# SSD mixer of a hybrid decoder trunk: the gate's product from PSUM, its norm in six calls, decayed x by ScalarE, and transposed b in one bank with c·b

## The chip, the core and the metric

One NeuronCore of a Trainium2 chip runs the whole program. It has TensorE (PE, matmuls, results in PSUM banks), VectorE (DVE), ScalarE (ACT), GpSimd (POOL, which does not touch PSUM here) and SyncE (SP, which issues DMAs here). Each engine runs its own instructions in order and waits for the others on semaphores. The metric is the device time of one execution in microseconds (us); lower is better.

## The reference

All arrays are float32. 1040 tokens (16 learned ones, then 1024) pass a Mamba-2 SSD mixer, a conv gated FFN, stick-breaking attention and a second FFN. The change is in the mixer:

```python
z, xbc, dt_raw = split(u @ w_in)
xbc = silu(causal_dwconv(xbc, conv_w, conv_b))
xs, b_in, c_in = split(xbc)            # 4 groups of 8 heads of 64; state 128
dt = softplus(dt_raw + dt_bias)
xdt = x_c * dt_c                       # per chunk and head
cb = einsum('bclgn,bcsgn->bgcls', c_c, b_c)
y_diag = einsum('bgcls,bgecls,bcsgep->bclgep', cb, decay_in, xdt)
decay_to_end = exp(a_cs[..., -1:] - a_cs)
chunk_states = einsum('bclgn,bgecl,bclgep->cbgepn', b_c, decay_to_end, xdt)
...                                    # scan over chunks, y_off from the states
y = y_diag + y_off + xs * d_skip
hg = y * silu(z)                       # the gate
hg = hg * rsqrt(mean(hg * hg over a group of 512) + eps)
out = (hg * gate_g) @ w_out
```

## The kernel before

Activations lie with channels on the partitions and tokens along the free axis, in three token tiles of 348, 348 and 344 (`TT`). The input projection is done by blocks of 128 channels: a *tile* is one block and one token tile, 24 matmuls into one PSUM bank (`project`, L153 to L155: each product is split into high and low parts). The bank is `pj`, of the pools `mm` (two banks) and `ex` (one), so that a bank comes back after three tiles. A tile of x, b or c then gets its conv: a first step by ScalarE (L275) and three by VectorE (L278), and Silu (L459). A tile of the gate gets Silu into an SBUF tile `z` (L491), the product with y (L498, `product`), the square (L503) and the sum of squares (L507, L509).

The SSD itself goes by four groups of heads (0 to 3) and nine chunks of up to 116 tokens (0 to 8). For a chunk, `ssd_decays` loads the cumulated decays into D and E by DMA, subtracts eight times on VectorE (L573) and takes the exponential on ScalarE (L574); `ssd_front` makes c·b (`cb`, L589), the transposed x (`px`, L592), the masked `cbm` (L595), `xdt` (L597), the decayed product D (L598), the transposed b (`pb`, L602) with its copy `bk` (L604), and the decayed x, `xde` (L606); `ssd_back` makes the chunk's state S from `bk` and `xde` (L619, L626) and y (L631, L633, L635). `cb`, `pb`, y and the norm's `ms` share the pool `sm` of three banks (a tag each allocation takes in turn), `px` and S the pool `lg` of two.

`mixer` writes the order by hand for all engines but the DMA queues: between a chunk's front and its back it puts the tiles of the next group's projection and of this group's gate (`stream`), about two a chunk in groups 0 and 3, and three or four in groups 1 and 2. Each chunk's decays are computed after the second tile of the chunk before. The gate of group g runs in group g+1; in that group, after its four blocks, `norm` is called at three tiles in a row, once for each token tile: `rstd` sums over partitions into a bank `ms` (L186), takes Ln and Exp on ScalarE (L189, L190) and one Newton step on VectorE (L191 to L194, of which L192 reads `ms`); `gate_norm` scales four blocks (L520).

Of the kernel before, what the change touches and what calls it, by code (L numbers as in the profile page):

```python
# [8 lines left out]
F32 = mybir.dt.float32  # L9
# [4 lines left out]
P = 128  # L14
# [52 lines left out]
class Trunk:  # L67
# [109 lines left out]
        self.tc.keep_in_program_order(self.nc.scalar.preload_act_table_set("natural_log_exp_and_others"))  # L177


    def rstd(self, accs, n, width, y=None, table=True):  # L180
        nc = self.nc
        if table:
            self.ln_exp()
        ps = self.sm("ms")
        for i, acc in enumerate(accs):
            nc.tensor.matmul(ps[:, :n], self.ones, acc[:, :n], start=i == 0, stop=i == len(accs) - 1)  # L186
        b = accs[0]
        y = self.tmp("y")[:, :n] if y is None else y
        nc.scalar.activation(y, ps[:, :n], AF.Ln, scale=1.0 / width)  # L189
        nc.scalar.activation(y, y, AF.Exp, scale=-0.5)  # L190
        nc.vector.tensor_tensor(b[:, :n], y, y, op=ALU.mult)  # L191
        nc.vector.tensor_tensor(b[:, :n], b[:, :n], ps[:, :n], op=ALU.mult)  # L192
        nc.vector.tensor_scalar(b[:, :n], b[:, :n], -0.5 / width, 1.5, op0=ALU.mult, op1=ALU.add)
        nc.vector.tensor_tensor(y, y, b[:, :n], op=ALU.mult)  # L194
        return y
# [185 lines left out]
    def dt_path(self, ps, r9, cp):  # L381

        nc, a = self.nc, self.a
        H, C = HEADS, 9 * HEADS
        heads = cp.tile([P, 2, H], F32, tag="heads", name="heads")
        nc.gpsimd.dma_start(heads.rearrange("p i h -> p (i h)"), a["heads"].to_broadcast([P, 2 * H]))
        aneg = heads[:, 1]
        self.tc.keep_in_program_order(nc.scalar.activation(aneg, aneg, AF.Exp))
        nc.vector.tensor_scalar(aneg, aneg, -1.0, None, op0=ALU.mult)

        G = 3 * H
        rows = self.tmp("rows")
        nc.gpsimd.memset(rows[:G, TT[2][1] : 3 * CB], 0.0)
        for j, (_, n) in enumerate(TT):
            nc.scalar.activation(rows[j * H : j * H + H, :n], ps[j * H : j * H + H, :n], AF.Copy)
        pv = self.sm("dt")
        for i in range(3):
            nc.tensor.transpose(pv[:CB, i * G : i * G + G], rows[:G, i * CB : i * CB + CB], self.ident[:G, :G])
        self.cols = cp.tile([P, 3, 9, H], F32, tag="cols", name="cols")
        R = slice(0, CB), slice(0, C)  # L400
        dt, acs, dte = (self.cols[:CB, i].rearrange("p c h -> p (c h)") for i in range(3))
        e, q, s, v = (self.tmp("dt")[R] for _ in range(4))
        tt, stt, ts = nc.vector.tensor_tensor, nc.vector.scalar_tensor_tensor, nc.vector.tensor_scalar

        bias = heads[:CB, 0].unsqueeze(1).to_broadcast([CB, 9, H])
        v3 = v.rearrange("p (c h) -> p c h", h=H)
        tt(v3, pv[R].rearrange("p (c h) -> p c h", h=H), r9[:CB].rearrange("p i j -> p (i j)").unsqueeze(2).to_broadcast([CB, 9, H]), op=ALU.mult)
        tt(v3, v3, bias, op=ALU.add)
        nc.scalar.activation(e, v, AF.Abs)
        nc.scalar.activation(e, e, AF.Exp, scale=-1.0)  # L410
        ts(q, e, 0.5, 1.0, op0=ALU.mult, op1=ALU.add)
        nc.vector.reciprocal(q, q)
        tt(s, e, q, op=ALU.mult)
        tt(e, s, s, op=ALU.mult)
        ts(q, e, 1.0 / (13 * 4**6), None, op0=ALU.mult)
        for c in (5, 4, 3, 2, 1):
            stt(q, q, 1.0 / ((2 * c + 1) * 4**c), e, op0=ALU.add, op1=ALU.mult)
        stt(q, q, 1.0, s, op0=ALU.add, op1=ALU.mult)
        stt(dt, v, 0.0, q, op0=ALU.max, op1=ALU.add)

        last = self.cols[:CB, 0, 8]
        nc.gpsimd.affine_select(out=last, in_=last, compare_op=ALU.is_ge, fill=0.0, base=CH[8][1] - 1, pattern=[[0, H]], channel_multiplier=-1)
        yield 1

        tt(e.rearrange("p (c h) -> p c h", h=H), self.cols[:CB, 0], aneg[:CB].unsqueeze(1).to_broadcast([CB, 9, H]), op=ALU.mult)
        pa, pe = self.sm("acs"), self.sm("end")
        nc.tensor.matmul(pa[R], self.past[:CB, :CB], e, start=True, stop=True)
        nc.tensor.matmul(pe[:, :C], self.ones[:CB, :], e, start=True, stop=True)
        nc.vector.tensor_copy(acs, pa[R])
        self.cd = cp.tile([P, 9, H], F32, tag="cd", name="cd")  # L430
        nc.scalar.activation(self.cd.rearrange("p c h -> p (c h)"), pe[:, :C], AF.Exp)
        tt(dte, pe[R], acs, op=ALU.subtract)
        nc.scalar.activation(dte, dte, AF.Exp)
        yield 2

        self.acs_d = self.dp.tile([9, H, CB], F32, tag="acs_d", name="acs_d")
        self.ea_d = self.dp.tile([9, H, CB], F32, tag="ea_d", name="ea_d")
        pr = self.sm("rows")
        for i in range(3):
            nc.tensor.transpose(pr[:G, i * CB : i * CB + CB], self.cols[:CB, 1, 3 * i : 3 * i + 3].rearrange("p c h -> p (c h)"), self.ident[:CB, :CB])  # L440
        ea = self.tmp("ea")
        nc.vector.tensor_copy(rows[:G, : 3 * CB], pr[:G, : 3 * CB])
        nc.scalar.activation(ea[:G, : 3 * CB], pr[:G, : 3 * CB], AF.Exp)
        for j in range(3):
            for d, t in ((self.acs_d, rows), (self.ea_d, ea)):
                nc.sync.dma_start(d[3 * j : 3 * j + 3].rearrange("c h l -> h c l"),
                                  t[j * H : j * H + H, : 3 * CB].rearrange("h (c l) -> h c l", l=CB))
        yield 3
# [29 lines left out]
        return [block(DI + (4 * g + q) * P, 4 * g + q) for q in range(4)] + [  # L478
            block(2 * DI + g * P, 16 + g), block(2 * DI + (GROUPS + g) * P, 20 + g)]

    def gate_group(self, u, g, x, acc, later):

        nc = self.nc
        tt = nc.vector.tensor_tensor
# [1 line left out]
        def block(q):  # L486
            def tile(w, j):
                s0, n = TT[j]
                ps = self.project(w, u, j, 0, bank=self.ex if j == 2 else None)
                z = self.tmp("z")  # L490
                nc.scalar.activation(z[:, :n], ps[:, :n], AF.Silu)  # L491
                self.settle()
                later(j, lambda: product(j, z))

            def product(j, z):
                s0, n = TT[j]
                xq = x[q][:, s0 : s0 + n]
                tt(xq, xq, z[:, :n], op=ALU.mult)  # L498
                self.open.append(lambda: square(j, z))

            def square(j, z):
# [10 lines left out]

        return [block(q) for q in range(4)]

    def gate_norm(self, g, x, acc, j):
        s0, n = TT[j]
        r = self.rstd([acc.pop(j)], n, DI // GROUPS)
        for q in range(4):
            xq = x[q][:, s0 : s0 + n]
            self.nc.vector.scalar_tensor_tensor(xq, xq, self.par("gate_norm", 4 * g + q), r, op0=ALU.mult, op1=ALU.mult)  # L520
# [7 lines left out]
    def stream(self, blocks, w0=None):  # L528
# [3 lines left out]
        todo = []  # L532
        for src, f in blocks:
            if src is None:
                for j in range(3):
                    calls[3 * len(todo) + 1 + j] = lambda f=f, j=j: f(j)
            else:
                todo.append((src, f))
# [41 lines left out]
    def ssd_front(self, g, x, bt, ct, c, dk, pool):  # L580
# [4 lines left out]
        t0, n = CH[c]  # L585
        cc = 3 * (c % 3) + c // 3
        e = t0 + n
        pcb = self.sm("cb")
        nc.tensor.matmul(pcb[:n, :n], bt[:, t0:e], ct[:, t0:e], start=True, stop=True)  # L589
        px = self.lg("px")  # L590
        for q in range(4):
            nc.tensor.transpose(px[:n, q * P : q * P + P], x[q][:, t0:e], self.ident)  # L592
        px = px[:n].rearrange("p (h d) -> p h d", h=GH)
        cbm = pool.tile([P, CB], F32, tag="cbm", name=self.nm("cbm"), bufs=2)
        tt(cbm[:n, :n], pcb[:n, :n], self.past[:n, :n], op=ALU.mult)  # L595
        xdt = pool.tile([P, GH, 64], F32, tag="xdt", name=self.nm("xdt"), bufs=2)
        tt(xdt[:n], px, self.cols[:n, 0, cc, h0 : h0 + GH].unsqueeze(2).to_broadcast([n, GH, 64]), op=ALU.mult)  # L597
        tt(dk, dk, cbm[:n, :n].unsqueeze(1).to_broadcast([n, GH, n]), op=ALU.mult)  # L598
        bk = xde = None
        if c < 8:  # L600
            pb = self.sm("pb")
            nc.tensor.transpose(pb[:n, :P], bt[:, t0:e], self.ident)  # L602
            bk = pool.tile([P, P], F32, tag="bk", name=self.nm("bk"), bufs=2)
            nc.scalar.activation(bk[:n], pb[:n, :P], AF.Copy)  # L604
            xde = pool.tile([P, GH, 64], F32, tag="xde", name=self.nm("xde"), bufs=2)
            nc.gpsimd.tensor_tensor(xde[:n], xdt[:n], self.cols[:n, 2, cc, h0 : h0 + GH].unsqueeze(2).to_broadcast([n, GH, 64]), op=ALU.mult)  # L606
        return xdt, xde, bk

    def ssd_back(self, g, x, c, dk, ce, xdt, xde, bk, state, pool):
# [29 lines left out]
    def mixer(self, mx):  # L639
# [5 lines left out]
        with self.tc.tile_pool(name="ssd", bufs=3) as pool:  # L645
# [8 lines left out]
                    waiting.append((j, f))  # L654

            def gate(g):
                def norm(j):
                    self.gate_norm(g, rows[g], accs[g], j)
                    if j == 2 and g < 2:
                        yd[g] = self.spill(rows[g][:4], f"y{g}_d")  # L660
                return self.gate_group(u, g, rows[g], accs[g], later if g == 3 else lambda j, f: f()) + [(None, norm)]

            into = lambda g: self.in_group(u, g, rows[g])
            blocks = into(1) + gate(0) + into(2) + gate(1) + into(3) + gate(2) + gate(3)
# [861 lines left out]
```

## Time and profile before

| | us |
|---|---|
| median of 3 runs | 3060.58 |
| runs from, to | 3060.25, 3062.45 |
| the profiled execution | 3064.0 |
| its span, first to last instruction | 3062.3 |
| TensorE busy | 2895.1 |
| VectorE busy | 2333.7 |
| ScalarE busy | 1650.2 |
| GpSimd busy | 1421.5 |

Line numbers are those of the kernel before. An engine is busy while an instruction of its own runs; waits are inferred from semaphore events. PEclk is the share of full speed that TensorE's clock was granted. The SSD groups run from 150 to 696 us of the span, and what follows is the output projection, the FFNs and the attention.

### The profile page before, as it was taken

How to read it: one execution, taken by the hardware profiler on the slowest of the kernel's cores; microseconds unless marked ns; L12 is line 12 of the kernel's file. 1: busy time of each engine (PE TensorE's matmuls, PEld its weight loads, DVE VectorE, ACT ScalarE, POOL GpSimd, SP SyncE). 2: the span in 40 equal slices, each digit the busy share in tenths (PEclk: the TensorE clock that was granted, in tenths of full speed). 3: DMA queues.
4: the chain of work that ended last, by engine and by line, in shares of the span. 5: the costliest groups of instructions: out<-in, count | busy, mean ns of one | idle time of the engine just before them, and what ended most of it. 6: DMA issues, size and time to landing. Idle time of an engine off the chain costs nothing. (4 is left out here: it accounts for less than half of the span.)

```text
span 3062.3 us, 58683 instructions
## 1 busy us (share of the span) xinstructions
PE 2895.1 (95%) x22535; PEld 2776.6 (91%) x22535; DVE 2333.7 (76%) x4030; ACT 1650.2 (54%) x3403; POOL 1421.5 (46%) x1289
## 2 busy tenths in 40 slices
PE   5999999989998999998999999999898999998997
PEld 2999898979998999998999999999797999998996
DVE  3686868885458888788966888888759878878874
ACT  3555545553245555554324888878635655565332
POOL 1154434452325766657643222223325666666741
PEclk8999999999998999999999999999998999999998
DMA  3333333324221222234132222221431222225231
GB/s 113 106 93 95 103 88 105 105 70 139 65 89 56 78 77 78 82 114 165 49 126 80 62 63 64 67 62 48 146 110 57 82 82 77 75 87 180 76 98 56
DMA packets 123220, 273.41 MB, mean 89 GB/s; under 512 B 13468, under 2 KB 53020, under 8 KB 122940
## 3 DMA queue, kind: packets, MB, share of 16 engines
q1 hardware_dynamic: 117622, 258.54, 27.3%
q10 hardware_dynamic: 4054, 6.56, 0.6%
q8 instruction: 177, 2.90, 0.4%
q0 software_dynamic: 1264, 4.57, 0.4%
q14 instruction: 103, 0.84, 0.1%
HBM read 201.25 MB, written 53.45 MB: 83 GB/s over the span
## 5 line engine op out<-in xcount | busy, mean ns | idle before, releaser
L153 PE MATMUL pj<-uh,wh 128*128 128x348 f32 (+2 forms) x1536 | 505.4, 329 | 9.0 <-ACT bk L604 6.2
L154 PE MATMUL pj<-ul,wh 128*128 128x348 f32 (+2 forms) x1536 | 497.6, 324 | 0.0
L155 PE MATMUL pj<-uh,wl 128*128 128x348 f32 (+2 forms) x1536 | 494.9, 322 | 0.7 <-POOL wl L1147 0.7
L154 PE MATMUL p<-bl,fh 128*128 128x262 f32 x1408 | 401.2, 285 | 14.0 <-DVE bl L814 14.0
L153 PE MATMUL p<-bh,fh 128*128 128x262 f32 x1408 | 402.2, 286 | 1.6 <-ACT fh L845 1.1
L155 PE MATMUL p<-bh,fl 128*128 128x262 f32 x1408 | 399.7, 285 | 0.0
L846 POOL TENSOR_TENSOR fl<-x,fh 128x1024 fp32r<-128x1024 f32 x88 | 212.7, 2418 | 353.0 <-ACT fh L845 276.3
L147 POOL TENSOR_TENSOR wl<-w,wh 128x1024 fp32r<-128x1024 f32 (+2 forms) x80 | 164.6, 2060 | 348.0 <-ACT wh L146 347.9
L154 PE MATMUL p<-bl,wh 128*128 128x262 f32 x1056 | 303.3, 287 | 8.6 <-DVE bl L814 8.6
L153 PE MATMUL p<-bh,wh 128*128 128x262 f32 x1056 | 302.0, 287 | 6.3 <-ACT bh L813 6.3
L153 PEld LDWEIGHTS pj<-uh,wh 128*128 128x128 f32 x1536 | 291.4, 190 | 14.4 <-issue 4.2
L155 PE MATMUL p<-bh,wl 128*128 128x262 f32 x1056 | 302.1, 286 | 0.0
L154 PEld LDWEIGHTS pj<-ul,wh 128*128 128x128 f32 x1536 | 292.0, 190 | 1.3 <-issue 0.7
L155 PEld LDWEIGHTS pj<-uh,wl 128*128 128x128 f32 x1536 | 291.5, 190 | 1.1 <-POOL wl L1147 1.0
L278 DVE SCALAR_TENSOR_TENSOR c<-p,params,c 128x260 f32<-128x260 f32 x528 | 251.3, 484 | 49.2 <-ACT c L275 39.1
L154 PEld LDWEIGHTS p<-bl,fh 128*128 128x128 f32 x1408 | 266.9, 190 | 16.1 <-DVE bl L814 15.9
L153 PE MATMUL acc<-gh,wh 128*128 128x260 f32 x896 | 260.1, 290 | 22.2 <-DVE p L1037 10.8
L154 PE MATMUL acc<-gl,wh 128*128 128x260 f32 x896 | 258.8, 289 | 12.4 <-DVE gl L992 12.4
L153 PEld LDWEIGHTS p<-bh,fh 128*128 128x128 f32 x1408 | 267.0, 190 | 3.7 <-ACT fh L845 1.5
L155 PEld LDWEIGHTS p<-bh,fl 128*128 128x128 f32 x1408 | 266.6, 190 | 0.1
L886 DVE TENSOR_TENSOR c<-c,c 128x260 f32<-128x260 f32 x176 | 254.1, 1445 | 6.6 <-ACT c L882 3.6
L155 PE MATMUL acc<-gh,wl 128*128 128x260 f32 x896 | 257.3, 288 | 0.6 <-POOL wl L990 0.6
(311 smaller groups left out, 8562.4 us busy)
## 6 DMA issues: line engine op xcount, KB each, us to landing
w<-in_w_up SPq DMA_DIRECT2D x88, 512.0 KB
g<-c SPq DMA_DIRECT2D x176, 130.0 KB
w<-in_w_down SPq DMA_DIRECT2D x44, 512.0 KB
w<-in_w_in SPq DMA_DIRECT2D x40, 512.0 KB
b<-g SPq DMA_DIRECT2D x32, 520.0 KB
E<-ea_d SPq DMA_DIRECT2D x32, 464.0 KB
D<-acs_d SPq DMA_DIRECT2D x32, 420.5 KB
h<-h_d SPq DMA_DIRECT2D x16, 520.0 KB
```

The source lines that it names most:

```text
L147: nc.gpsimd.tensor_tensor(wl[:, :n], w32[:, :n], wh[:, :n].bitcast(F32), op=ALU.subtract)
L153: mm(out, wh, uh, start=first, stop=False, skip_group_check=joins)
L154: mm(out, wh, ul, start=False, stop=False, skip_group_check=joins)
L155: mm(out, wl, uh, start=False, stop=last, skip_group_check=joins)
L278: nc.vector.scalar_tensor_tensor(out, ps[:, o + i : o + i + n], wcol(i), out, op0=ALU.mult, op1=ALU.add)
L846: tt(lo[:, :n], t, hi[:, :n].bitcast(F32), op=ALU.subtract)
L886: self.last_up = tt(g[:, :FN], g[:, :FN], v[:, :FN], op=ALU.mult)
```

## The change

Five edits, cut to their core:

```diff
-    def rstd(self, accs, n, width, y=None, table=True):
+    def rstd(self, accs, n, width, y=None, table=True, early=False):
...
-        ps = self.sm("ms")
+        ps = bank = self.sm("ms")
...
         nc.scalar.activation(y, ps[:, :n], AF.Ln, scale=1.0 / width)
+        if early:
+            ps = self.tmp("ms")
+            nc.scalar.activation(ps[:, :n], bank[:, :n], AF.Copy)
...
         nc.scalar.activation(dte, dte, AF.Exp)
+        tt(dte, dte, dt, op=ALU.mult)
...
-                z = self.tmp("z")
+                z = ps if now else self.tmp("z")
                 nc.scalar.activation(z[:, :n], ps[:, :n], AF.Silu)
...
                 tt(xq, xq, z[:, :n], op=ALU.mult)
+                z = self.tmp("z") if now else z
...
-                for j in range(3):
+                for j in range(6):
                     calls[3 * len(todo) + 1 + j] = lambda f=f, j=j: f(j)
...
-        pcb = self.sm("cb")
-        nc.tensor.matmul(pcb[:n, :n], bt[:, t0:e], ct[:, t0:e], start=True, stop=True)
+        both = self.sm("cb")
+        pcb, pb = both[:n, :n], both[:n, P : 2 * P]
+        bk = xde = None
+        if c < 8:
+            nc.tensor.transpose(pb, bt[:, t0:e], self.ident)
+            bk = pool.tile([P, P], F32, tag="bk", name=self.nm("bk"), bufs=2)
+            nc.scalar.activation(bk[:n], pb, AF.Copy)
+        nc.tensor.matmul(pcb, bt[:, t0:e], ct[:, t0:e], start=True, stop=True)
...
-            nc.gpsimd.tensor_tensor(xde[:n], xdt[:n], self.cols[:n, 2, cc, h0 : h0 + GH].unsqueeze(2).to_broadcast([n, GH, 64]), op=ALU.mult)
+            for i in range(GH):
+                nc.scalar.activation(xde[:n, i], px[:, i], AF.Copy, scale=self.cols[:n, 2, cc, h0 + i : h0 + i + 1])
...
-                def norm(j):
-                    self.gate_norm(g, rows[g], accs[g], j)
-                    if j == 2 and g < 2:
+                r = {}
+
+                def norm(i):
+                    j = i // 2
+                    if i % 2 == 0:
+                        r[j] = self.rstd([accs[g].pop(j)], TT[j][1], DI // GROUPS, early=True)
+                    else:
+                        self.gate_norm(g, rows[g], j, r.pop(j))
+                    if i == 5 and g < 2:
```

For the gates of groups 0 to 2 (`now`, g < 3) Silu writes back into its PSUM bank and the product reads it there. The norm is called at six tiles in a row, `rstd` and `gate_norm` by turns, and a copy of `ms` to SBUF stands behind Ln. `xde` is made from `px` by eight scaled copies on ScalarE, with dt taken into the scale once, ahead of the groups. Transposed b and c·b share a bank, and transposed b comes first.

TensorE at the front of group 0's chunk 6 (`y` is the end of chunk 5, `pj` the next tile), before:

```order
L633 MATMUL y_1883<-E_1712,state_1762 64x116
L589 MATMUL cb_1905<-xbc_1074,xbc_977 116x116 [waits PE_49]
L592 MATMUL px_1907<-ident,xbc_530 116x128 [waits PE_49]
...
L592 MATMUL px_1907<-ident,xbc_880 116x128
L602 MATMUL pb_1917<-ident,xbc_977 116x128
L153 MATMUL pj_1930<-uh_127,wh_1716 128x352
```

and in the changed program, whose line numbers are some lines higher, and where the first `cb` row is the transposed b:

```order
L642 MATMUL y_1920<-E_1743,state_1793 64x116
L599 MATMUL cb_1942<-ident,xbc_978 116x128 [waits PE_49]
L602 MATMUL cb_1942<-xbc_1075,xbc_978 116x116 [waits Activation_49]
L605 MATMUL px_1947<-ident,xbc_530 116x128 [waits PE_49]
...
L605 MATMUL px_1947<-ident,xbc_881 116x128
L153 MATMUL pj_1973<-uh_127,wh_1747 128x352
```

Transposed b moved from the last place to the first, and the c·b matmul behind it, L602, holds a wait on ScalarE that L589 had not.

ScalarE at the same place, before (conv of the tile ahead, Silu, the decays' exponential, the copy of transposed b):

```order
L275 ACTIVATE xbc_1720<-pj_1839,params 128x344 [waits PE_49]
L459 ACTIVATE xbc_1720<-xbc_1720 128x348 [waits DVE_49]
L574 ACT_TABLE_LOAD [waits DMAHW0_49]
L574 ACTIVATE D_1835<-D_1835 116x928 [waits DVE_49]
L604 ACTIVATE bk_1919<-pb_1917 116x128 [waits PE_49,Activation_49]
L146 ACTIVATE wh_1925<-w_258_1923 128x1024 [waits DMAHW2_49,Pool_49]
```

and in the changed program:

```order
L279 ACTIVATE xbc_1751<-pj_1876,params 128x344 [waits PE_49]
L465 ACTIVATE xbc_1751<-xbc_1751 128x348 [waits DVE_49]
L581 ACT_TABLE_LOAD [waits DMAHW0_49]
L581 ACTIVATE D_1872<-D_1872 116x928 [waits DVE_49]
L601 ACTIVATE bk_1944<-cb_1942 116x128 [waits PE_49,Activation_49]
L615 ACTIVATE xde_1957<-px_1947,cols 116x64 [waits DVE_49,Activation_49]
L615 ACTIVATE xde_1957<-px_1947,cols 116x64 x7
L146 ACTIVATE wh_1968<-w_251_1966 128x1024 [waits DMAHW2_49,Pool_49]
```

The copy keeps its place behind the exponential; the eight copies to `xde` are new, and the first waits for VectorE.

VectorE at the first norm of group 0's gate, in group 1 (`z` and `y` are the norm's tiles, `xbc` with `pj` a conv), before:

```order
L191 TENSOR_TENSOR z_2308<-y_2877 128x348 [waits PE_49,Activation_49]
L192 TENSOR_TENSOR z_2308<-z_2308,ms_2875 128x348 [waits DVE_49]
...
L194 TENSOR_TENSOR y_2877<-y_2877,z_2308 128x348 [waits DMAHW7_49,DMAHW6_49,DVE_49]
L520 SCALAR_TENSOR_TENSOR xbc_530<-xbc_530,params,y_2877 128x348 [waits DVE_49]
...
L520 SCALAR_TENSOR_TENSOR xbc_880<-xbc_880,params,y_2877 128x348
L278 SCALAR_TENSOR_TENSOR xbc_2841<-pj_2888,params,xbc_2841 128x348 [waits Activation_49]
```

and in the changed program:

```order
L195 TENSOR_TENSOR z_2366<-y_2950 128x348 [waits PE_49,Activation_49]
L196 TENSOR_TENSOR z_2366<-z_2366,ms_2952 128x348 [waits DVE_49]
...
L198 TENSOR_TENSOR y_2950<-y_2950,z_2366 128x348 [waits DMAHW7_49,DMAHW6_49,DVE_49]
L282 SCALAR_TENSOR_TENSOR xbc_2914<-pj_2959,params,xbc_2914 128x348 [waits Activation_49]
...
L611 TENSOR_TENSOR D_2865<-D_2865,cbm_3025 116x928 [waits DVE_49]
L527 SCALAR_TENSOR_TENSOR xbc_530<-xbc_530,params,y_2950 128x348
```

The four scalings moved behind the next tile's conv and the chunk's front, and `ms` is now the copy in SBUF.

More of the change, by code (lines that the diff above doesn't have):

```diff
@@ L479, in in_group, with gate_group @@
             block(2 * DI + g * P, 16 + g), block(2 * DI + (GROUPS + g) * P, 20 + g)]
-    def gate_group(self, u, g, x, acc, later):
+    def gate_group(self, u, g, x, acc, later, now):
         nc = self.nc
@@ L513, in gate_group, with gate_norm @@
         return [block(q) for q in range(4)]
-    def gate_norm(self, g, x, acc, j):
+    def gate_norm(self, g, x, j, r):
         s0, n = TT[j]
-        r = self.rstd([acc.pop(j)], n, DI // GROUPS)
         for q in range(4):
@@ L594, in ssd_front @@
         cbm = pool.tile([P, CB], F32, tag="cbm", name=self.nm("cbm"), bufs=2)
-        tt(cbm[:n, :n], pcb[:n, :n], self.past[:n, :n], op=ALU.mult)
+        tt(cbm[:n, :n], pcb, self.past[:n, :n], op=ALU.mult)
         xdt = pool.tile([P, GH, 64], F32, tag="xdt", name=self.nm("xdt"), bufs=2)
@@ L598, in ssd_front @@
         tt(dk, dk, cbm[:n, :n].unsqueeze(1).to_broadcast([n, GH, n]), op=ALU.mult)
-        bk = xde = None
         if c < 8:
[L601 to L604, printed above, removed]
             xde = pool.tile([P, GH, 64], F32, tag="xde", name=self.nm("xde"), bufs=2)
-            nc.gpsimd.tensor_tensor(xde[:n], xdt[:n], self.cols[:n, 2, cc, h0 : h0 + GH].unsqueeze(2).to_broadcast([n, GH, 64]), op=ALU.mult)
+            for i in range(GH):
+                nc.scalar.activation(xde[:n, i], px[:, i], AF.Copy, scale=self.cols[:n, 2, cc, h0 + i : h0 + i + 1])
         return xdt, xde, bk
@@ L656, in gate @@
             def gate(g):
-                def norm(j):
-                    self.gate_norm(g, rows[g], accs[g], j)
-                    if j == 2 and g < 2:
+                r = {}
[6 more added lines that the diff above has]
+                    if i == 5 and g < 2:
                         yd[g] = self.spill(rows[g][:4], f"y{g}_d")
-                return self.gate_group(u, g, rows[g], accs[g], later if g == 3 else lambda j, f: f()) + [(None, norm)]
+                return self.gate_group(u, g, rows[g], accs[g], later if g == 3 else lambda j, f: f(), g < 3) + [(None, norm)]
             into = lambda g: self.in_group(u, g, rows[g])
```

## The prediction

> **What bounds the kernel now.** I read the page first, then the stretches by stage, then the waits of TensorE inside the stretch that the change touches, and last the timeline of single chunks.
>
> ```profile
> core 0: 3062.3 us, clock 0.978
> PE 2895.1 (95%) x22535; PEld 2776.6 (91%) x22535; DVE 2333.7 (76%) x4030; ACT 1650.2 (54%) x3403; POOL 1421.5 (46%) x1289
> ...
> core 0: us, PE busy (x) PEld busy (x) DVE busy (x) ACT busy (x) POOL busy (x), PEclk, DMA share, GB/s
> 150.00:255.20 105.20, 105.20 (x818) 97.56 (x817) 85.39 (x191) 58.05 (x80) 53.08 (x29) 1.00 0.33 97
> 255.20:412.70 157.50, 151.61 (x1078) 142.60 (x1077) 120.73 (x248) 82.43 (x118) 67.50 (x37) 0.97 0.34 96
> 412.70:569.70 157.00, 150.73 (x1078) 141.24 (x1077) 117.45 (x232) 80.36 (x119) 66.61 (x37) 0.98 0.35 100
> 569.70:696.00 126.30, 113.17 (x852) 103.03 (x852) 110.60 (x211) 68.83 (x100) 64.02 (x32) 0.97 0.28 80
> ```
>
> TensorE is busy for 95% of the span. The four stretches are the four SSD groups, 150 to 696 us, in which alone the change moves work: in group 0 TensorE never stops and has its full clock; in groups 1 to 3 it lacks 5.9, 6.3 and 13.1 us. VectorE is close behind (88% busy in group 3). So what the change can win is TensorE's idle time there, and the time lost to its slower clock:
>
> ```profile
> PE pb L602 <- DVE z L192: 6.9, 3, 2.6
> PE ms L186 <- ACT bk L604: 6.6, 3, 5.8
> PE pj L153 <- ACT bk L604: 6.2, 2, 3.2
> PE S L619 <- POOL xde L606: 4.0, 4, 1.2
> PE y L631 <- DVE D L598: 1.5, 1, 1.5
> ...
> 323.44:326.86 3.42, 0.93 (x4) 0.62 (x4) 3.25 (x7) 2.75 (x5) 2.41 (x2) 1.00 0.91 283
> 326.86:330.28 3.42, 3.42 (x13) 3.28 (x12) 3.35 (x7) 1.59 (x3) 0.00 (x0) 0.50 0.28 88
> ```
>
> Columns of the waits: us in total, times, longest. They sum to 25.2 us. The first three are the norm of the gate: its PSUM bank `ms` comes free only when VectorE reads it at L192, and three norms in three tiles overfill VectorE. The last two rows show what a stall costs besides itself: TensorE worked 0.93 of 3.42 us, and in the next 3.42 us the granted clock was 0.50, which loses 1.7 us.
>
> **The change part by part.**
>
> *What goes.* All 25.2 us of waits, and the clock: 0.03 x 157.5 + 0.02 x 157.0 + 0.03 x 126.3 = 11.6 us, of which some lies on the idle time itself; I take 10. Together 35 us, the most that can be won. The norm in six calls halves VectorE's load per tile, and `ms` is freed by one ScalarE copy right after Ln, so the first three rows should go; `pb` has no bank of its own any more; `xde` no longer waits for GpSimd. I count 33, leaving 2 us for remnants.
>
> *What comes: a new wait on TensorE.* Before, transposed b (`pb`) had its own bank, and TensorE went on to the projections while ScalarE copied it to `bk`; only the state matmul S, two to four tiles later, needed `bk`. Now `pb` and `cb` share a bank, `pb` is written first, and in the changed program every `cb` matmul after a copy waits for a ScalarE instruction, which is `bk` (chunk 8, which has no `bk`, lacks that wait). TensorE is in order: `cb`, `px` and the next tile's 24 matmuls stand behind it. Nothing covers it. So each of 31 chunks pays from the end of `pb` to the end of `bk`. When is `bk` done? Group 0, chunk 6:
>
> ```profile
> 219.75 0.64 ACT L275 ACTIVATE xbc<-pj,params 128x344 f32<-128x344 f32 x1 [1.39 <-PE pj L155]
> 220.42 1.80 DVE L278 SCALAR_TENSOR_TENSOR xbc<-pj,params,xbc 128x344 f32<-128x344 f32 x3 [0.51 <-ACT xbc L275]
> 222.14 2.38 DVE L573 TENSOR_SCALAR D<-D,cols 116x116 f32<-116x116 f32 x8
> 222.30 0.46 PE L589 MATMUL cb<-xbc,xbc 128*116 128x116 f32 x2
> 223.03 0.27 PE L602 MATMUL pb<-ident,xbc 128*116 128x128 f32 x1
> 224.56 0.98 ACT L574 ACTIVATE D<-D 116x928 f32<-116x928 f32 x1 [2.48 <-DVE D L573]
> 225.44 0.26 ACT L604 ACTIVATE bk<-pb 116x128 f32<-116x128 f32 x1
> ...
> 233.61 0.46 PE L589 MATMUL cb<-xbc,xbc 128*116 128x116 f32 x2
> 236.62 0.26 ACT L604 ACTIVATE bk<-pb 116x128 f32<-116x128 f32 x1
> ```
>
> `bk` stands on ScalarE behind the decay's exponential (L574), which waits for VectorE's eight subtractions (L573), which stand behind the conv of the tile that TensorE finished just before. This chain starts when the tile ends and is no backlog: VectorE had waited 0.51 us for that tile's first ScalarE step. `pb`, now first, would end near 222.40, `bk` ends at 225.70: 3.3 us; in the next chunk 233.71 to 236.88, 3.2 us. By durations alone (conv 0.64 + 1.80, subtractions 1.60 as undisturbed below, exponential 0.98, copy 0.26: 5.3 from the conv's start at 219.75, against 2.65 from there to the end of `pb`) it is 2.6. I take 3.0 for the 7 chunks that pay: 21 us. The order of these steps on ScalarE and VectorE is not changed.
>
> Groups 1 and 2 have three or four tiles a chunk, and the exponential is done a tile earlier:
>
> ```profile
> 273.67 0.27 PE L602 MATMUL pb<-ident,xbc 128*116 128x128 f32 x1
> 273.98 0.28 ACT L604 ACTIVATE bk<-pb 116x128 f32<-116x128 f32 x1 [0.76 <-PE pb L602]
> ...
> 303.42 0.27 PE L602 MATMUL pb<-ident,xbc 128*116 128x128 f32 x1
> 305.33 0.27 ACT L604 ACTIVATE bk<-pb 116x128 f32<-116x128 f32 x1
> ```
>
> The first is the floor, 0.6 us from `pb`'s start: ScalarE stood ready. The second is 2.2 us, with 0.65 us more as `pb` now comes first. Of 16 chunks I put 8 at 0.6 and 8 (first chunks, and those under the norm) at 2.5: 25 us. Group 3 has two gate tiles a chunk:
>
> ```profile
> 604.28 2.48 DVE L498 TENSOR_TENSOR xbc<-xbc,z 128x344 f32<-128x344 f32 x1
> 604.47 0.46 PE L589 MATMUL cb<-xbc,xbc 128*116 128x116 f32 x2
> 606.68 1.60 DVE L573 TENSOR_SCALAR D<-D,cols 116x116 f32<-116x116 f32 x8
> 609.20 0.26 ACT L604 ACTIVATE bk<-pb 116x128 f32<-116x128 f32 x1
> ...
> L498 DVE TENSOR_TENSOR xbc<-xbc,z 128x348 f32<-128x348 f32 (+1 forms) x48 | 58.6, 1224 | 14.9 <-ACT z L491 14.9
> L192 DVE TENSOR_TENSOR z<-z,ms 128x348 f32<-128x348 f32 (+1 forms) x12 | 6.2, 513 | 0.3
> ```
>
> Here 604.57 to 609.46 would be 4.9 us. But 2.48 of it is the gate's product, which now reads PSUM, as L192 does in 0.51: less 2.0 that leaves 2.9, and I take 2.2, nearer the floor, since a stall of TensorE also drains VectorE's backlog: 8 times, 18 us. Bounds per chunk 0.6 (the floor) to 4.9. Sum of new waits: 64 us.
>
> *Half clock after the new stalls.* The pair of windows above is the nearest row: 2.5 us idle in one window, half clock in the next. Fifteen stalls (7 at 3.0, 8 at 2.5) come near it; how much falls into one window is chance, so I take 0.6 x 15 x 1.7 = 15 us; ends 0 and 23 x 1.7 = 39. The Trainium skill ("TensorE: Matmul & The Clock Gate", HAM oscillation) sets the limit at idle gaps above about 3.4 us; by it this term would be 0 and the time 3092. The trace disagrees: no listed wait of VectorE's `z` was above 2.6 us, and the clock fell.
>
> *The product from PSUM.* 36 of 48 products go from 1.22 to 0.51 us: 26 us of VectorE. It hides in VectorE's waits save where counted above; `pj` is held until the product, and a bank is needed again three tiles later.
>
> *`xde` on ScalarE.*
>
> ```profile
> L606 POOL TENSOR_TENSOR xde<-xdt,cols 116x512 f32<-116x512 f32 x32 | 59.6, 1862 | 198.2 <-DVE xdt L597 176.1 <-DMA E<-ea_d 22.1
> L1156 ACT ACTIVATE wh<-w,params 128x128 fp32r<-128x128 f32 x168 | 55.4, 446 | 0.0
> L194 DVE TENSOR_TENSOR y<-y,z 128x348 f32<-128x348 f32 (+1 forms) x12 | 10.2, 851 | 0.4
> ```
>
> Eight scaled copies of 64 columns a chunk. The nearest row copies 128 columns with a column as scale at 55.4/168 = 0.33 us each; half as wide I take 0.26, so 2.1 us a chunk (bounds 1.0 and 2.6) and 67 us of ScalarE, which is idle for over 40% of each group. In group 0 the copies end before the next tile does, so I charge nothing. But the first of them waits for VectorE's `xdt` from the same bank: the 176.1 us for which GpSimd stood still, at no cost to others, are now ScalarE's, with the next tiles' Silu and conv behind it. I charge 0, since the new stall gives VectorE time to catch up; the other end is a rival below. In return GpSimd loses 59.6 us, and with it collisions with VectorE.
>
> *Small things.* Twelve copies of `ms` (about 0.5 us each, as L192 reads that bank) and one more table load lie in ScalarE's idle time; L192 now reads SBUF and may take 0.85 as L194: 4 us of VectorE, covered by the spread. The last group's norms come after TensorE has gone on to the output projection. One more VectorE multiply ahead of the groups runs beside conv work: 0. Two E and D loads swap on SP's queue, with three D buffers as cover: 0.
>
> **The sum.** -33 + 64 + 15 = +46. The profiled execution took 3064.0 us over a span of 3062.3; the median of the runs shown is 3060.6, 0.1% lower, and I forecast against that: 3107 us. With ends: 7 x 2.6 + 24 x 0.6 = 33, no half clock, less 35: -2. And 7 x 3.3 + 8 x 0.6 + 8 x 4.0 + 8 x 4.9 = 99, plus 39, less 30: +108.
>
> The Trainium skill ("PSUM — Partial Sum Buffer", Summary: rules for kernel authors) advises to read PSUM in another bank than the one a matmul writes; the shared bank of `pb` and `cb` goes against it, and no run of before shows the price.
>
> **The rivals.**
>
> *Faster: the wait stays at its floor.* If `bk` came after 0.6 us everywhere, as at 273.98, the new waits were 31 x 0.6 = 19 us, without half clock: -35 + 19 = -16, 3045 us. It decides at 35/31 = 1.1 us a chunk. Against it stands group 0, where the chain from the tile's end alone takes 21 us.
>
> *No change: the waits change their name.* If VectorE bounds groups 1 to 3 anyway, the new waits there take the place of the old ones and only group 0's 18 us count, of which the won clock gives back 12: 3061 to 3067.
>
> *Much slower: ScalarE stuck behind `xdt`.* GpSimd's wait was 176.1 us over 30 chunks, 5.9 each. On ScalarE it makes Silu and conv start late, banks come free late, and VectorE wait for ScalarE in its turn. ScalarE's idle time covers the first part of it; if 40% reached TensorE, 70 us on the sum: 3177. It decides where the lateness exceeds the two tiles for which a projection bank can wait. For it speaks that VectorE is 88% busy in group 3, against it that in group 0 `xdt` follows `bk` at once.
>
> **How the numbers follow.** A measurement tells 0.2%, 6 us, from no change. Chances: the forecast, slower between 3067 and 3168, 0.82; much slower 0.08; no change 0.05; faster 0.05. The range 3072 to 3168 runs from near the low end of the sum to below the last rival, and leaves out 0.2.
>
> **What would show it.** Right: a wait of TensorE's `cb` on ScalarE's `bk`, some 31 times and about 64 us, the longest total in the SSD stretch; group 0 about 30 us longer with a granted clock below 1.00; the product near 0.5 us; no waits on `z` at the norm. Wrong: `cb` waits under 30 us in all, or ScalarE idle on `xdt` for over 100 us with projections waiting for banks.

## The result, and the profile after

The changed kernel takes 3157.75 us (median of 4 runs, 3154.41 to 3161.73) against 3061.31 us before: a ratio of 1.0311, 95% interval 1.0296 to 1.0327. It is 96 us slower; 46 were forecast.

The first lines of the page, the waits of TensorE from 150 to 800 us (us in total, times, longest), and the four SSD groups as stretches, each from its first `cb` bank to the next group's, the last to the end of its `y`:

```profile
core 0: 3157.1 us, clock 0.970
PE 2920.0 (92%) x22535; PEld 2796.0 (89%) x22535; DVE 2287.7 (72%) x4031; ACT 1707.2 (54%) x3672; POOL 1359.5 (43%) x1257
...
PE cb L602 <- ACT bk L601: 95.7, 31, 11.7
...
core 0: us, PE busy (x) PEld busy (x) DVE busy (x) ACT busy (x) POOL busy (x), PEclk, DMA share, GB/s
146.07:292.73 146.66, 124.28 (x856) 115.30 (x853) 87.18 (x197) 73.96 (x148) 38.40 (x21) 0.91 0.25 74
292.73:474.20 181.47, 154.85 (x1078) 144.80 (x1077) 105.98 (x248) 96.63 (x185) 51.79 (x29) 0.92 0.29 84
474.20:648.27 174.07, 152.19 (x1078) 142.14 (x1076) 103.42 (x233) 95.07 (x186) 51.53 (x29) 0.95 0.31 91
648.27:782.11 133.84, 109.00 (x790) 99.37 (x788) 79.06 (x190) 77.53 (x156) 42.57 (x22) 0.94 0.24 72
```

Of the five kinds of wait of before none is left: TensorE waits for one thing, 31 times. The same stretches of the kernel before:

```profile
151.61:255.17 103.56, 103.56 (x808) 95.92 (x807) 84.54 (x189) 57.53 (x79) 53.08 (x29) 1.00 0.33 97
255.17:412.66 157.49, 151.60 (x1078) 142.59 (x1077) 120.76 (x248) 82.42 (x118) 67.50 (x37) 0.97 0.34 96
412.66:569.65 156.99, 150.72 (x1078) 141.23 (x1076) 117.41 (x232) 80.35 (x119) 66.61 (x37) 0.98 0.35 100
569.65:685.92 116.27, 103.14 (x789) 93.14 (x788) 103.64 (x201) 65.45 (x94) 60.09 (x30) 0.97 0.28 83
```

The groups end 37.6, 61.5, 78.6 and 96.2 us later than before; what follows them is no longer than it was (2375.0 against 2376.4 us). Group 0, which had no idle TensorE and its full clock, now has 22.4 us of idle time and a clock of 0.91. In the clock's record the SSD stretch has 26 windows of 3.41 us at half clock, before 7.

A regular chunk of group 0 in the changed kernel, and the windows around it:

```profile
202.10 1.60 DVE L580 TENSOR_SCALAR D<-D,cols 116x116 f32<-116x116 f32 x8
202.28 0.32 PE L599 MATMUL cb<-ident,xbc 128*116 128x128 f32 x1
203.74 0.98 ACT L581 ACTIVATE D<-D 116x928 f32<-116x928 f32 x1 [1.70 <-DVE D L580]
204.62 0.26 ACT L601 ACTIVATE bk<-cb 116x128 f32<-116x128 f32 x1
204.93 0.46 PE L602 MATMUL cb<-xbc,xbc 128*116 128x116 f32 x2 [2.33 <-ACT bk L601]
...
202.89:206.31 3.42, 1.38 (x11) 1.38 (x12) 3.12 (x12) 1.14 (x2) 0.00 (x0) 1.00 0.78 176
206.31:209.72 3.41, 3.41 (x13) 3.41 (x13) 1.28 (x2) 2.69 (x9) 0.30 (x1) 0.50 0.28 88
```

This is the forecast mechanism, in its order: subtractions, exponential, `bk`, and only then `cb` (L599 is the transposed b, L602 the c·b). TensorE stands still for 2.33 us and the next window is at half clock. The dearest chunk, chunk 6 of group 1, has another cause ahead of `bk`:

```profile
404.42 4.17 DVE L527 SCALAR_TENSOR_TENSOR xbc<-xbc,params,y 128x344 f32<-128x344 f32 x4
407.19 2.32 POOL L361 DMA_DIRECT2D y_d<-xbc  x4
411.25 0.32 PE L599 MATMUL cb<-ident,xbc 128*116 128x128 f32 x1
415.67 0.64 ACT L279 ACTIVATE xbc<-pj,params 128x348 f32<-128x348 f32 x1 [11.28 <-DMA y_d<-xbc]
418.07 1.60 DVE L580 TENSOR_SCALAR D<-D,cols 116x116 f32<-116x116 f32 x8
422.93 0.26 ACT L601 ACTIVATE bk<-cb 116x128 f32<-116x128 f32 x1
423.24 0.73 PE L602 MATMUL cb<-xbc,xbc 128*116 128x116 f32 x2 [11.66 <-ACT bk L601]
```

The norm's last scalings (L527) end at 408.6, GpSimd issues the spill of the four finished rows (L361), and ScalarE's next conv writes a row buffer that this spill must have read: it stands for 11.28 us, with the exponential and `bk` behind it and TensorE behind `bk`. Two rows of ScalarE's waits (150 to 800 us), one of them this, and three groups of the same stretch:

```profile
ACT xde L615 <- DVE xdt L610: 90.5, 32, 6.4
...
ACT xbc L279 <- DMA y_d<-xbc: 19.1, 2, 11.3
...
L615 ACT ACTIVATE xde<-px,cols 116x64 f32<-116x64 f32 x256 | 55.8, 329 | 90.5 <-DVE xdt L610 90.5
L505 DVE TENSOR_TENSOR xbc<-xbc,pj 128x348 f32<-128x348 f32 (+1 forms) x36 | 18.3, 509 | 35.7 <-ACT pj L498 35.7
L196 DVE TENSOR_TENSOR z<-z,ms 128x348 f32<-128x348 f32 (+1 forms) x9 | 9.3, 1037 | 0.3
```

### The profile page after: what moved, and what is told of

Same layout as the page of the kernel before. It is cut to its first block, busy times and chain, and to the rows that moved or that the text cites. A ratio compares the mean times of both kernels' runs of the same rounds, so it can differ in the third digit from the quotient of the medians.

```text
span 3157.1 us, 58932 instructions
## 1 busy us (share of the span) xinstructions
PE 2920.0 (92%) x22535; PEld 2796.0 (89%) x22535; DVE 2287.7 (72%) x4031; ACT 1707.2 (54%) x3672; POOL 1359.5 (43%) x1257
## 4 chain that ended last, share of the span: by engine, by line
PE 70%; DVE 14%; issue 5%; ACT 4%; DMA 4%; POOL 1%; SPq 0%; POOLq 0%; ACTq 0%; DVEq 0%
PE p L153 9%; PE p L154 9%; PE p L155 9%; PE pj L153 6%; PE pj L154 6%; PE pj L155 6%; PE acc L153 5%; PE acc L154 5%; PE acc L155 5%; PE po L1311 2%; DVE gl L1007 2%; PE lg L1270 2%; PE wT L1297 2%; DVE D L580 1%; DMA x<-in_x 1%
## 5 line engine op out<-in xcount | busy, mean ns | idle before, releaser
L153 PE MATMUL pj<-uh,wh 128*128 128x348 f32 (+2 forms) x1536 | 512.2, 334 | 2.7 <-DVE xbc L282 1.6
L153 PEld LDWEIGHTS pj<-uh,wh 128*128 128x128 f32 x1536 | 297.9, 194 | 7.4 <-issue 3.9
```

The source lines that it names most:

```text
L153: mm(out, wh, uh, start=first, stop=False, skip_group_check=joins)
```

## The experiments

All ratios are to the kernel before, run beside them on the same chip. Two theories stood after the result. "Wait": `cb` behind `bk`, and the half clock that follows. "ScalarE": the copies to `xde` and their wait for `xdt` (90.5 us) hold ScalarE up, and `bk` is only where it shows.

### One part undone, one part alone

**own_bank**, the changed kernel:

```
-        both = self.sm("cb")
-        pcb, pb = both[:n, :n], both[:n, P : 2 * P]
+        pcb = self.sm("cb")[:n, :n]
         if c < 8:
+            pb = self.sm("pb")[:n, :P]
```

> The changed kernel, with transposed b in a bank of its own again (still first), all else of the change kept. Theory 'wait': the slowdown is TensorE's cb standing behind ScalarE's bk (95.7 us in the changed kernel's SSD stretch) and the half clock after it (44 us lost there against 12 us before). Then both go: no wait of cb on bk, clock in group 0 back at 1.00, time 3030 to 3070 us. Theory 'ScalarE': the eight scaled copies and their wait for xdt (90.5 us) hold ScalarE, and bk is only where it shows. Then the time stays above 3110 us, with projections waiting for banks in place of cb.

**xde_gpsimd**, the changed kernel (and `dte` is not multiplied by `dt`):

```
-            for i in range(GH):
-                nc.scalar.activation(xde[:n, i], px[:, i], AF.Copy, scale=...)
+            nc.gpsimd.tensor_tensor(xde[:n], xdt[:n], self.cols[...], op=ALU.mult)
```

> The changed kernel, with xde back on GpSimd (from xdt), the shared bank kept. Theory 'wait': bk stands behind the exponential, the conv of the norm's tiles and the spill, none of which is xde's: cb still waits 75 us or more, time 3130 to 3165 us. Theory 'ScalarE': ScalarE comes to bk in time, cb waits under 40 us, time below 3100 us.

**b_shared**, the kernel before with only the change's first lines of `ssd_front` (`both`, transposed b, `bk`, `cb`):

> The kernel before, with the shared bank and transposed b first alone; product, norm and xde as before. Theory 'wait': this edit alone brings the slowdown: from the start of cb to the end of bk the kernel before shows 142 us over 32 chunks, of which the 25 us of old waits and the drained backlog take a part; cb waits 75 to 130 us, time 3125 to 3190 us. Theory 'ScalarE': without the copies on ScalarE the wait is near its floor, 0.6 us a chunk, 19 us: 3061 to 3085 us.

**b_xde**, the kernel before with only the eight copies:

> The kernel before, with xde as eight scaled copies on ScalarE alone. Theory 'wait': nothing on TensorE waits for them, 3050 to 3075 us, although ScalarE stands idle for xdt over 80 us. Theory 'ScalarE': 3100 us or more.

| kernel | median, us | before, us | ratio | 95% |
|---|---|---|---|---|
| own_bank | 3090.85 | 3063.91 | 1.0087 | 1.0070 to 1.0104 |
| xde_gpsimd | 3155.74 | 3063.91 | 1.0299 | 1.0284 to 1.0315 |
| b_shared | 3146.79 | 3063.91 | 1.0277 | 1.0256 to 1.0297 |
| b_xde | 3092.68 | 3063.91 | 1.0091 | 1.0076 to 1.0106 |

TensorE's waits in the four, in this order (first rows of each, 140 to 850 us):

```profile
PE ms L187 <- ACT bk L601: 21.1, 3, 9.5
PE S L628 <- ACT xde L615: 9.4, 4, 2.7
...
PE cb L601 <- ACT bk L600: 91.3, 31, 9.0
...
PE cb L595 <- ACT bk L594: 86.0, 31, 11.5
...
PE pb L603 <- DVE z L192: 10.8, 5, 3.0
PE S L621 <- ACT xde L608: 10.4, 5, 3.4
```

The wait alone brings 83 of the 96 us, and without `xde` on ScalarE the changed kernel is no faster beyond the intervals. So "ScalarE" is wrong as the cause. Nor is it the new place of transposed b: own_bank keeps it first, without the stall, and costs what b_xde costs with the old order (1.0087 and 1.0091). But "wait" missed own_bank and b_xde too: with no stall of `cb`, `xde` on ScalarE costs 29 us by itself. S waits for it, and other waits of TensorE grow (in all 48 us in the groups of b_xde, against 26 before), so that its groups are 5.0, 5.4, 6.4 and 9.4 us longer. The two costs do not add up in the changed kernel: 83 and 29 would be 112, and it lost 96.

### The order in the bank, and what the rest is worth

**copy_behind**, the changed kernel with `bk`'s copy behind both products:

```
             nc.tensor.transpose(pb, bt[:, t0:e], self.ident)
-            bk = pool.tile([P, P], F32, tag="bk", ...)
-            nc.scalar.activation(bk[:n], pb, AF.Copy)
         nc.tensor.matmul(pcb, bt[:, t0:e], ct[:, t0:e], start=True, stop=True)
+        if c < 8:
+            bk = pool.tile([P, P], F32, tag="bk", ...)
+            nc.scalar.activation(bk[:n], pb, AF.Copy)
```

> The changed kernel with the two products of the shared bank back to back, and bk's copy behind both: one bank, no wait of cb. Theory 'wait': the shared bank costs nothing in itself; without the wait in the middle the time is at most that of transposed b in its own bank (3090.9 us), and since a bank of the three is free the 21 us for which ms waited for a bank held by bk there shrink too: 3060 to 3085 us, what is left being xde's. Theory 'bank' (the sharing itself costs, as ScalarE and VectorE read while TensorE writes): 3110 us or more.

**one_bank_gpsimd**, the same with `xde` on GpSimd:

> As the kernel with bk's copy behind both products in one bank, and with xde back on GpSimd: what is left of the change is the product from PSUM, the norm in six calls with the early copy, and the one bank. Theory 'two costs' (the wait of cb, and xde's wait for xdt on ScalarE, worth 29 us alone): both are gone, and part of the 35 us of old waits and half clock is won: 3030 to 3058 us, faster than both kernels. Theory 'VectorE bounds the groups': 3058 to 3070 us, as the old waits come back under other names.

**b_product_norm**, the changed kernel with `ssd_front` and `dte` as before:

> The kernel before with the product from PSUM and the norm in six calls with its early copy; banks and xde as before. If these two do what the prediction counted (33 us): 3025 to 3040 us. If the norm's bank still waits behind bk (cb, pb, ms and y share three banks): 3040 to 3065 us, with a wait of ms on bk of 10 us or more.

| kernel | median, us | before, us | ratio | 95% |
|---|---|---|---|---|
| copy_behind | 3086.03 | 3063.65 | 1.0070 | 1.0055 to 1.0085 |
| one_bank_gpsimd | 3063.72 | 3063.65 | 0.9997 | 0.9988 to 1.0006 |
| b_product_norm | 3068.62 | 3063.65 | 1.0014 | 1.0004 to 1.0023 |

The waits of the three (TensorE's, and one row of ScalarE's in the second):

```profile
PE pj L153 <- DVE xbc L282: 19.8, 8, 5.9
PE S L629 <- ACT xde L616: 15.5, 8, 3.2
...
PE pj L153 <- DVE xbc L282: 22.6, 9, 7.1
ACT xbc L279 <- DMA y_d<-xbc: 22.6, 2, 11.3
...
PE ms L187 <- ACT bk L610: 23.3, 3, 10.8
```

copy_behind came out 1 us above its range and far from "bank": the shared bank shows no price of its own. With both products written before anyone reads it costs no more than two banks (1.0070 against 1.0087, intervals that overlap), and `ms` finds a bank free. So one line's place is most of the loss: moved behind both products it leaves 22 of 96 us, and with `xde` on GpSimd nothing of 92 (xde_gpsimd against one_bank_gpsimd). What is left in copy_behind is again the price of `xde` on ScalarE, 22 us here. On the Trainium skill's advice ("PSUM — Partial Sum Buffer", Summary: rules for kernel authors), weighed in the prediction: what the runs price is the wait that guards the bank, and an order in which both writes come before the reads pays none.

My gain did not come, either: one_bank_gpsimd went the rival's way, product, norm and one bank are worth nothing together (0.9997), and product and norm with the old banks lose 0.1%, a little above the range of the second case, by the wait that it names. The 25 us of old waits come back under other names, as the last three rows show: projections wait for the conv, the conv for the spill's DMA, or `ms` for a bank that `bk` holds. The six calls put the last scaling, and with it the spill, three tiles later, just ahead of the conv that needs the row; the kernel before has no wait of a conv on that DMA.

### The half clock

**px_fill**, the changed kernel with `px` between transposed b and `cb`, done six times over:

```
+        px = self.lg("px")
+        for q in 6 * tuple(range(4)):
+            nc.tensor.transpose(px[:n, q * P : q * P + P], x[q][:, t0:e], self.ident)
         nc.tensor.matmul(pcb, bt[:, t0:e], ct[:, t0:e], start=True, stop=True)
```

> The changed kernel, wait and all, with px's four transposes ahead of cb and done six times over (the same values into the same bank), so that TensorE works for some 2 us of each wait of cb on bk. Theory 'clock by busy share' (a window of 3.41 us in which TensorE is busy under half is followed by one at half clock): bk comes no earlier, but most waits of 2.3 us no longer fall under half a window; of the 44 us lost to the clock in the SSD stretch 20 us or more come back, and 0.4 us a chunk from px standing in the wait: 3115 to 3135 us. Theory 'clock by gap length' (only gaps above 3.4 us lower the clock): the waits of 4 to 12 us alone count, which the filling leaves above or just below that limit: half clock falls by under 10 us, 3135 to 3150 us.

Measured: 3147.18 us, ratio 1.0270 (1.0253 to 1.0287). Its four groups as stretches:

```profile
146.05:284.27 138.22, 133.02 (x1037) 124.59 (x1034) 86.46 (x197) 73.88 (x148) 38.46 (x21) 0.99 0.27 79
284.27:464.19 179.92, 170.40 (x1258) 161.14 (x1256) 105.03 (x248) 96.64 (x185) 51.48 (x29) 0.97 0.31 85
464.19:642.59 178.40, 168.02 (x1259) 159.28 (x1257) 104.25 (x241) 95.23 (x186) 51.44 (x29) 0.98 0.31 88
642.59:768.03 125.44, 120.36 (x970) 111.04 (x968) 78.28 (x183) 76.96 (x154) 44.16 (x22) 1.00 0.27 77
```

The mechanism is shown: 6 windows at half clock in place of 26, a loss of 10 us in place of 44, with `bk` no earlier; by gap length under 10 us were to come back. The time missed the first theory's range and fell into the other's, since I forgot what the filling costs where the wait is short: in 18 chunks `cb` now starts 2.78 us after transposed b, though `bk` was there or nearly so, and the ninth chunks are filled for nothing. Group 0, where each wait is above 2 us, shows the gain best: 138.2 against 146.7 us.

### The norm and its spill

**after_three**, the changed kernel with the norm of before (three calls, no early copy):

> The changed kernel with the norm as before, in three calls without the early copy; shared bank and xde on ScalarE kept. Theory 'spill': the six calls put the spill of the normed rows three tiles later, and ScalarE's conv into the row buffer that it frees waits for its DMA (19.1 us in the changed kernel's SSD stretch, none before), with bk behind it and TensorE's cb behind that: without it the waits of chunk 6 (11.7 and 8.2 us) fall to 3 us or less: 3135 to 3150 us, if the norm that now comes at once does not give as much back. Theory 'norm at once is worse': VectorE's three norms in three tiles hold the exponential and so bk as much: 3150 to 3175 us.

**three_calls**, the same norm in the one-bank kernel with `xde` on GpSimd:

> The kernel with both products in one bank, bk's copy behind them and xde on GpSimd (3063.7 us, equal to before), with the norm in three calls as before. Left of the change: product from PSUM, one bank. Theory 'spill': its waits of the conv on the spill's DMA (22.6 us, twice 11.3) go, and the old wait of pb on the norm cannot come back since pb has no bank of its own: 3035 to 3057 us. Rival 'VectorE': the norm at once fills VectorE and the conv waits as long: 3057 to 3070 us.

**four_calls**, the one-bank kernel with each tile's scaling in the call of the next tile's mean square:

```
 def norm(i):
     if i < 3:
         now = self.rstd([accs[g].pop(i)], TT[i][1], DI // GROUPS, early=True)
     if i:
         self.gate_norm(g, rows[g], i - 1, r.pop(i - 1))
```

> The same one-bank kernel with the norm in four calls (the next tile's mean square in the same call as this tile's scaling), with the early copy: the spill leaves two tiles (some 9 us) earlier than with six. Theory 'spill': conv waits for its DMA under 5 us in all, 3035 to 3055 us. Rival 'VectorE': 3057 to 3070 us.

**four_spill**, that kernel with the rows spilled tile by tile:

> As the kernel with four calls, and the rows are spilled tile by tile behind each scaling, twelve DMAs in place of four, so that only a third is left to write behind the last. Theory 'spill': no wait on it at all, 3033 to 3053 us, and at most 3 us below the four calls. Rival 'issue': the twelve DMA issues on GpSimd (0.55 us each) hold E's product and the weights' low parts: 3 to 10 us above the four calls.

| kernel | median, us | before, us | ratio | 95% |
|---|---|---|---|---|
| after_three | 3165.79 | 3065.17 | 1.0327 | 1.0304 to 1.0350 |
| three_calls | 3058.51 | 3065.17 | 0.9978 | 0.9968 to 0.9987 |
| four_calls | 3061.36 | 3065.17 | 0.9986 | 0.9975 to 0.9997 |
| four_spill | 3060.98 | 3065.17 | 0.9986 | 0.9975 to 0.9996 |

TensorE's first wait in after_three, and its first two in three_calls:

```profile
PE cb L603 <- ACT bk L602: 95.5, 31, 14.3
...
PE pj L153 <- ACT bk L603: 6.4, 2, 3.2
PE ms L187 <- DVE z L196: 5.3, 3, 1.9
```

In after_three the spill's wait is gone and chunk 6 waits 1.8 us in both groups, not 11.7 and 8.2; but chunk 5 now waits 14.3 us in each, not 7.2, as the whole norm stands ahead of the subtractions. The sum is 95.5 us again, and the second theory's range held: while `cb` waits for `bk`, the norm's time reached TensorE in both places in which it was put. In the one-bank kernel the theory 'spill' failed in all three, as the times lie above its ranges: the waits on its DMA are gone, but others stand in their place (the last two rows). three_calls and four_calls came out in the rival's range; four_spill in neither, as its rival 'issue' asked for 3 to 10 us above four_calls and it lies 0.4 us below. Against one_bank_gpsimd's 0.9997, three calls come to 0.9978, four calls and the spill by tiles to 0.9986; only the interval of three_calls lies clear of it. three_calls, with the product from PSUM and the one bank left of the change, beats both kernels, the one before by 6.7 us of 3065. Which of the two brings this was not separated.

## Why the prediction was right or wrong

*Direction and cause: right; the size of the cost: wrong.* `cb` waits for `bk` 31 times, the longest total, and b_shared and copy_behind show that this wait decides. Of the signs that I named, the clock below 1.00 in group 0, no wait on `z` at the norm and the product (0.51 us) came; group 0 ended 37.6 us later, not about 30, and ScalarE waited 90.5 us on `xdt`, not over 100. The loss was 96 us where I had 46: 32 us of the difference are waits of `cb`, 17 are half clock.

*The size of the waits: 64 forecast, 95.7 measured; the largest error.* By group, from the gaps before each `cb`:

| term | forecast, us | measured, us |
|---|---|---|
| group 0, 7 chunks | 21 | 22.4 |
| groups 1 and 2, 16 chunks | 25 | 48.5 |
| group 3, 8 chunks | 18 | 24.8 |

The step that failed is "first chunks, and those under the norm at 2.5". Chunks 5 and 6 of the two groups cost 7.2, 11.7, 7.2 and 8.2 us, 34.3 in all, where I had put 10, and each lies above 4.9, my upper bound for a chunk; the other twelve chunks cost 14.2, and I had 14.8. The trace before already had the lag, in chunk 5 of group 1:

```profile
344.10 0.27 PE L602 MATMUL pb<-ident,xbc 128*116 128x128 f32 x1
347.46 4.01 DVE L573 TENSOR_SCALAR D<-D,cols 116x116 f32<-116x116 f32 x8
354.73 0.26 ACT L604 ACTIVATE bk<-pb 116x128 f32<-116x128 f32 x1
```

`bk` ends 10.9 us after the start of `pb` there; in chunks 5 and 6 of both groups the trace before has 10.9, 4.2, 11.6 and 5.4 us, 32.0 in all. I let the norm in six calls take that lag away. It only split it differently over two chunks (in after_three, with three calls, the same four cost 32.3 us), and added the wait on the spill, which the prediction does not have: I counted the moved scalings and forgot the four DMAs behind them. In group 3 the product did fall to 0.51 us, but the chunks stayed at 1.7 to 5.1 us, 3.1 in the mean, where I took 2.2 as nearer the floor. In group 0 the pieces were wrong and their sum came right by luck: four chunks at 2.33 to 2.35, below the 2.6 that I had worked out, and three at 3.7, 4.7 and 4.7. The 2.6 is partly a wrong reading: I let `pb` end 0.10 us after it starts, where its row lasts 0.27 us before and 0.32 us now, which makes it 2.4 to 2.5. One of the last:

```profile
184.58 3.92 DVE L580 TENSOR_SCALAR D<-D,cols 116x116 f32<-116x116 f32 x8
185.14 2.15 POOL L584 TENSOR_TENSOR E<-E,xbc 128x928 f32<-128x928 f32 x1
189.73 0.54 PE L602 MATMUL cb<-xbc,xbc 128*116 128x116 f32 x1 [4.67 <-ACT bk L601]
```

One of the eight subtractions takes 2.17 us in place of 0.27 while GpSimd's product runs, the first takes 0.69 beside GpSimd's instruction ahead of it, and all of it reaches TensorE (4.67 against 2.33 us). The Trainium skill ("SBUF — State Buffer", Terms: shared port pair) says that of VectorE and GpSimd the loser is blocked for the whole instruction; the trace agrees, 3.92 against 1.60 us.

*Half clock: 15 forecast, some 32 measured, the second term that was too small.* 26 windows lose 44.4 us (0.09, 0.08, 0.05 and 0.06 of the stretches), of which some 12 lie in the idle time itself. I took 15 stalls, each with a chance of 0.6 of one window; there were 21 stalls of 1.7 us or more, 17 of them were followed by half clock, and after the long ones it lasted two to four windows.

*What goes: -33 forecast, -35 measured, by luck.* The 25.2 us of waits are gone, and with them the clock's 9.9 (7 windows lost 11.9 us, 2.0 of it in idle time). But they went because TensorE now stood elsewhere; one_bank_gpsimd, in which it does not, gains nothing from product and norm. For this part the rival "the waits change their name" was right. A small term was off too: the norm's step that now reads the SBUF copy (L196) takes 1.04 us, where I had put 0.85.

*`xde`: 0 charged.* Within this kernel that holds (3157.75 and 3155.74 us, with ratios whose intervals overlap), but by luck: what hides it is the stall, not idle ScalarE. Alone it costs 29 us, so the mechanism of "much slower" was real, at less than half its price. Nor is it hidden in every kernel with the stall: after_three, which is b_shared with the product from PSUM and `xde` on ScalarE, lost more (1.0327 against 1.0277, intervals apart); which of the two edits brings this was not separated. Each copy takes 0.33 us, not 0.26, but they start 0.20 us apart: 1.74 us a chunk, within my bounds.

By these sizes the sum is -35 + 96 + 32 = +93, against the 96 measured; 3 us stay unexplained.

## What to carry to other kernels

Two results that share a PSUM bank should both be written before either is read: the copy put between them here made TensorE wait for whatever stood ahead of that copy on the copying engine, a norm, a collision or a DMA elsewhere in the program included. A lag that costs nothing in a trace because it is covered is the price to use, row by row, once an edit takes the cover away; a mean over "chunks like these" hides the few that matter. A moved step brings its DMAs along, and the buffer that those free is due later too.

## What the runs showed of the hardware

In these traces the clock follows TensorE's busy share in windows of 3.41 us, and not the length of one gap. In the changed kernel between 100 and 3000 us, of the windows at full clock with TensorE busy under 0.4 of the time all 19 are followed by one at half clock, of those from 0.4 to 0.5 six of seven, above 0.5 none of 779. In px_fill it is 10 of 10, four of seven and none of 803; in one_bank_gpsimd one of four between 0.5 and 0.6 was, so the limit lies near a half, not at a sharp value. So a stop of 2.33 us (0.68 of a window) is enough if it falls into one window. The Trainium skill's rule ("TensorE: Matmul & The Clock Gate", HAM oscillation), that idle gaps above about 3.4 us are what to avoid, is too mild here; its window of that length (Part 1: The HAM clock gate) agrees with the record.

Not tried: the wait of `cb` taken away with the copy left in the middle, since the two products and the copy then meet in one bank unguarded.
